# A hybrid decoder block on one core: expert weights in 32 KB ring pieces, the state scan in one tile, constants and squares on VectorE

## The chip, the cores and the metric

The kernel runs on one core of a Trainium2 chip. The metric is the device time of one execution in microseconds (us). Its arithmetic is on TensorE (PE in the profile), VectorE (DVE), ScalarE (ACT) and GpSimd (POOL); SyncE (SP) issues nearly all of its DMAs.

## The reference

256 tokens of 2048 channels, all in float32, pass one decoder layer. What matters of it:

```python
h = rms_norm(x, g1);  proj = h @ w_in              # 1024 + 3*1024 + 2*2048 columns
# state-space mixer: 64 groups of 16 channels, 64 complex states each
x_t = abar * x_{t-1} + bbar @ u_t;  y_t = Re(c @ x_t) + d * u_t
out_s = (z * sigmoid(z @ w_glu)) @ w_bs            # z = gelu(y)
out_a = stick_breaking_attention(q, k, v) @ w_ba   # 8 heads of 128
x2 = x + (sigmoid gates merge out_s and out_a) @ w_out
h2 = rms_norm(x2, g2)
# 32 experts in 4 groups: the best group, in it the best two experts of each token
for e in range(32):
    out += combine[:, e] * (silu(h2 @ w_gate[e]) * (h2 @ w_up[e])) @ w_down[e]
return x2 + out
```

## The kernel before, in words

**The dense stage.** Everything up to `x2` is a list of 200 steps. Each step loads 512 KB of weights (`raw`, issued on SP five steps ahead), splits them into a high part `wh` (a cast on ScalarE) and a low part `wl` (a subtraction on VectorE), and does twelve 128x512 matmuls, `wh` with the high and low part of the activations and `wl` with the high part. All else in this stage is written as generators, `init_stats`, `attention`, `ssm`, `scan`, `gelu` and `heads`; after each step's matmuls the loop at L903 to L934 lets them issue a little, as estimated loads of the engines (`Meter`, L45) allow. Instructions of an engine run in the order in which this loop writes them.

**Three places in it that the change touches.** `init_stats` (L464) sums the squares of `x` over channels: three VectorE reductions leave three partial sums `xsq`, and 12 products with a column of ones (L487) add the partial sums and the partitions at once; each shows as two records. `ssm` (L523) builds the constants of the state space: products of 128x512 between `BC` and small vectors, some issued on GpSimd (`tt` without an engine, L535) and some on VectorE, into `BBD` and `CBD`, and PE transposes `BBD` into `BT`. `scan` (L502) is the recurrence over time. The even times are handled outside; 127 positions remain, and each needs a product of the previous state (real and imaginary parts, times two coefficients) and two additions. The 64 groups of states lie in two tiles `Vs`, and the loop alternates between the halves: two products of 128x64, four additions of 128x32 for a position.

**The expert stage.** The router picks experts; each expert has room for 32 tokens (a rarely used loop handles what overflows). An expert has 16 rows of `wgu` (gate and up) and 8 rows of `wd` (down), a row being 128 partitions x 4 KB, 512 KB. `load_piece` (L856) brings them in pieces of four rows, 2 MB, 16 KB for a partition: 192 pieces for 32 experts. They go round a ring of ten or eleven buffers of 16 KB for a partition, most of which serve as working space of the dense stage earlier. The first seven pieces are issued row by row among the weight loads of the dense stage (`ahead`), the eighth at step 196, and eleven can be in or on their way before the first is used. After that, `gate_up` (L1098) and `down` (L1126) call `load_piece` each time they have used up a piece:

```python
if used[0] <= held.get(j, -1):
    return
held[j] = n
```

For every group of four experts, `gather` (L1058) collects their tokens and `scatter` (L1141) adds the results into `accv`. The last two experts' gate/up weights come first, then their four down pieces, the last of them in two halves; `keep_busy` (L959) puts dummy transposes on PE ahead of those pieces (24 before each group of four gate/up rows, and 24 before each of the first two down pieces).

**The router's start.** When a quarter `n` of the columns of `x2` is done, `x2_tr` (L380) transposes it into a PSUM tile `ps`, ScalarE copies that to `xt` for the router's matmuls, and the squares of `x2` are summed for the norm: by ScalarE for the first three quarters, by VectorE for the fourth. Both write their squares into a scratch tile `junk` that nobody reads.

Of the kernel before, what the change touches and what calls it, by code (L numbers as in the profile page):

```python
# [17 lines left out]
P = 128  # L18
# [64 lines left out]
def hybrid_block(ctx, tc, A, out):  # L83
# [7 lines left out]
    U = {i: ctx.enter_context(tc.tile_pool(name=f"u{i}", bufs=1)) for i in range(11) if i != 6}  # L91

    def unit(i, shape, dt, name):
        return U[i].tile(shape, dt, name=name, tag="u")

    def slot(h, shape, dt, name):
        return hp.tile(shape, dt, name=name, tag=f"h{h}")
# [5 lines left out]
    hp = wctx.enter_context(tc.tile_pool(name="hp", bufs=1))  # L103
# [57 lines left out]
    uge = cq.tile([P, P], F32, name="uge")  # L161
# [5 lines left out]
    nmask = cq.tile([P, P], F32, name="nmask")  # L167
# [149 lines left out]
    def glu_fin(n):  # L317
        def f(a):
            if n == 0:
                ys = unit(7, [P, 2, 8, T], F32R, "ys")  # L320
                S["ys"] = (ys[:, 0], ys[:, 1])
# [58 lines left out]
    def x2_tr(n, t):  # L380
        ps = bg_tile(0)
        for i in range(4):
            k = 4 * n + i
            pe.transpose(ps[:, P * i:P * i + P], S["x2"][:, t, P * k:P * k + P], ident)
        xt = S["xt2"][n, t] = slot((2 * n + t) % 4, [P, 4, P], F32, "xt2")
# [75 lines left out]
    xsq01 = slot(0, [P, 2, T], F32, "xsq01")  # L461
    xsq = [xsq01[:, 0], xsq01[:, 1], slot(1, [P, T], F32, "xsq2")]

    def init_stats():  # L464
# [3 lines left out]
        for at, j, red in ((4, 0, None), (6, 1, (0, 0, 8)), (9, 2, (1, 8, 12)), (12, 3, (2, 12, 16))):  # L468
# [30 lines left out]
    coef = [cq.tile([P, 2, 2, 16], F32, name=f"coef{h}") for h in range(2)]  # L499
    prod = [cq.tile([P, 2, 2, 16], F32, name=f"prod{h}") for h in range(2)]  # L500

    def scan(Vs):  # L502
        at = [1, 1]
        while ("V", 0) not in prog:
            yield 0
        yield -1
        while min(at) < P:
            on = [h for h in range(2) if ("V", h) in prog and at[h] < P]
            for h in on:
                X, c = Vs[h], at[h]  # L510
                vec.tensor_tensor(prod[h], X[:, :, :, c - 1][:, :, None, :].to_broadcast([P, 2, 2, 16]), coef[h], op=OP.mult)
            for k in range(2):
                for h in on:
                    X, c = Vs[h], at[h]
                    vec.tensor_tensor(X[:, :, :, c], X[:, :, :, c], prod[h][:, k], op=OP.add)
            for h in on:
                at[h] += 1
            if len(on) == 1:
                load["vec"] += 0.4
            yield 1 if on else 0  # L520
        prog["scan"] = True

    def ssm():  # L523
        SE = pool
        sm_all = unit(7, [P, 128, 32], F32, "sm")
        sm = sm_all[:, 0:40]
        tw = [sm_all[:, 48 + 16 * i:64 + 16 * i].rearrange("p a b -> p (a b)").rearrange("p (a b) -> p a b", b=16) for i in range(5)]
# [70 lines left out]
        for h in range(2):  # L598
            hs = slice(16 * h, 16 * h + 16)
            SE.tensor_copy(coef[h][:, 0, 0], a2r[:, hs])  # L600
            SE.tensor_copy(coef[h][:, 0, 1], a2i[:, hs])
            SE.tensor_scalar(coef[h][:, 1, 0], a2i[:, hs], -1.0, None, op0=OP.mult)
            SE.tensor_copy(coef[h][:, 1, 1], a2r[:, hs])
# [18 lines left out]
        tt(tw[0], Bi, bc(ci), OP.mult)  # L622
        tt(tw[1], Br, bc(ci), OP.mult)
        yield 0
        tt(t1, Br, bc(cr), OP.mult, vec)
        tt(bre, t1, tw[0], OP.subtract, vec)
        tt(tw[2], Ci, bc(ai), OP.mult)
        yield 0
        tt(t2, Bi, bc(cr), OP.mult, vec)
        tt(bim, t2, tw[1], OP.add, vec)  # L630
        tt(tw[3], Ci, bc(ar), OP.mult)
        yield 0
        tt(tw[0], bim, bc(ai), OP.mult)
        tt(tw[1], bre, bc(ai), OP.mult)
        tt(t1, Cr, bc(ar), OP.mult, vec)
        for g in range(2):
            act.copy(diag(BBD, 0, g), part(bre, g))
            tt(diag(CBD, 2, g), part(t1, g), part(tw[2], g), OP.subtract, vec)
        yield 0
        tt(t2, Cr, bc(ai), OP.mult, vec)  # L640
        for g in range(2):
            act.copy(diag(BBD, 1, g), part(bim, g))
            vec.scalar_tensor_tensor(diag(CBD, 3, g), part(t2, g), -1.0, part(tw[3], g), op0=OP.mult, op1=OP.subtract)
        yield 0
        tt(t1, bre, bc(ar), OP.mult, vec)
        for g in range(2):
            tt(diag(BBD, 2, g), part(t1, g), part(tw[0], g), OP.subtract, vec)
            act.copy(diag(CBD, 0, g), part(Cr, g))
        yield 0
        tt(t2, bim, bc(ar), OP.mult, vec)  # L650
        for g in range(2):
            tt(diag(BBD, 3, g), part(t2, g), part(tw[1], g), OP.add, vec)
            act.mul(diag(CBD, 1, g), part(Ci, g), -1.0)
# [11 lines left out]
        CB = cq.tile([P, 16, 32], F32, name="CB")  # L665
# [17 lines left out]
        Vs = [unit(7 + h, [P, 2, 16, P], F32, f"Vs{h}") for h in range(2)]  # L683
        gens.append(scan(Vs))
        gens.append(gelu())
        for b in range(8):
# [7 lines left out]
            for i in range(2):  # L694
                src = tiles[i].rearrange("p (a r c) -> p r a c", a=2, r=2)
                j = 4 * (b % 4) + i
                act.copy(Vs[b // 4][:, :, j:j + 3:2], src)
# [6 lines left out]
        for b in range(8):  # L704
            pp = [bg_tile(0), bg_tile(0)]
            X = Vs[b // 4]
            for par in (1, 0):
                ps = pp[par]
                for si in range(3):
                    for j in range(4):  # L710
# [6 lines left out]
                        elif par == 1:  # L717
                            pe.matmul(ps[js, 0:P], CBD[:, si - 1, 4 * b + j], X[:, si - 1, i],
                                      start=False, stop=(si == 2), tile_position=(0, 32 * j))
                        else:  # L720
                            pe.matmul(ps[js, 1:P], CBD[:, 1 + si, 4 * b + j], X[:, si - 1, i, 0:P - 1],
# [5 lines left out]
    def gelu():  # L727
# [4 lines left out]
        zz = unit(9, [P, 2, 8, T], F32R, "zz")  # L732
# [28 lines left out]
    def attention():  # L761
# [20 lines left out]
        QT = [slot(h, [P, 2, T], F32, f"qkT{h}") for h in range(8)]  # L782
# [11 lines left out]
        AT = unit(4, [P, 2, 2, 2, 3, P], F32, "AT")  # L794
        gens.insert(0, heads(QT, AT[:, 0], (0, 2)))
        gens.insert(1, heads(QT, AT[:, 1], (4, 6)))

    def heads(QT, at, firsts):
# [4 lines left out]
        for h0 in firsts:  # L803
# [32 lines left out]
            for i in range(2):  # L836
                y = slot(h0 + i, [P, 2, T], F32R, f"ya{h0 + i}")
# [8 lines left out]
    ring = [U[i] for i in (10, 8, 9, 2, 7, 4, 3, 1)]  # L846
    used = [0]
    held = {}
    ahead = []
    pieces = [(e, i) for e in range(NE - 2) for i in range(6)]  # L850
    pieces += [(e, i) for e in (NE - 2, NE - 1) for i in range(4)]
    pieces += [(e, i) for i in (4, 5) for e in (NE - 2, NE - 1)]
    ptile = {}
    nextp = [0]

    def load_piece():  # L856
        n = nextp[0]
        if n >= len(pieces):
            return
        j = n % 11 if n < 22 else (n - 22) % 10  # L860
        j += n >= 22 and j > 5
        if used[0] <= held.get(j, -1):
            return
        held[j] = n
        e, i = pieces[n]
# [414 lines left out]
```

## Time and profile before

| | us |
|---|---|
| median of 3 runs | 1563.29 |
| lowest and highest | 1561.04, 1563.48 |
| the profiled execution's own time | 1564.15 |
| its span in the profile | 1562.4 |

| engine | busy us | share of the span |
|---|---|---|
| PE | 1263.4 | 81% |
| VectorE | 541.0 | 35% |
| ScalarE | 451.4 | 29% |
| GpSimd | 55.9 | 4% |

516.91 MB move in the span. All shares are averages over two stages that differ: the dense stage up to 633 us and the expert stage after it. So they are read by stretches: which engine is full in each, and what ended the idle time of the others.

### The profile page before, as it was taken

Reading aid. Unit: us, or ns where it says so; the run is one execution under the profiler, and the core shown is the slowest. Engines: PE = TensorE matmul, PEld = TensorE weight load, DVE = VectorE, ACT = ScalarE, POOL = GpSimd, SP = SyncE. Lnnn points to the kernel's source line nnn. Section 1 sums busy time; section 2 is a strip of 40 time slices with the busy share of each in tenths; the row PEclk is TensorE's granted clock in tenths of the full one; section 3 lists DMA queues with packets and bytes.
Section 4 is the critical chain, followed back from the end, with each engine's and each line's share of the span. In section 5 each row is a group of like instructions: output and inputs, shape, how many; then the busy total and the mean of one; then the engine's idle time right before and its main releaser. Section 6 shows DMA issues by size and latency. Waiting matters only on the chain.

```text
span 1562.4 us, 25151 instructions
## 1 busy us (share of the span) xinstructions
PE 1263.4 (81%) x10662; PEld 862.0 (55%) x10662; DVE 541.0 (35%) x1338; ACT 451.4 (29%) x768; POOL 55.9 (4%) x111
## 2 busy tenths in 40 slices
PE   9999999999999999987558557657657657657697
PEld 7878888888879888644224224323324323323364
DVE  7746878898856744302002002002002002001001
ACT  5645567554455444120100100110110110110101
POOL 6700000000000000000000000000000000000000
PEclk9999999999999999999879878878988779878899
DMA  8545655566657886999999999999999999999996
GB/s 266 175 131 159 195 153 158 163 193 189 202 191 256 277 281 229 379 427 427 427 427 428 428 426 426 428 428 427 427 427 427 426 428 428 426 428 427 426 426 242
DMA packets 65108, 516.91 MB, mean 331 GB/s; under 512 B 7905, under 2 KB 8161, under 8 KB 41441
## 3 DMA queue, kind: packets, MB, share of 16 engines
q1 hardware_dynamic: 64704, 515.21, 83.9%
q8 instruction: 86, 1.41, 0.4%
q14 instruction: 30, 0.24, 0.0%
q10 hardware_dynamic: 288, 0.06, 0.0%
HBM read 513.14 MB, written 2.10 MB: 330 GB/s over the span
## 4 chain that ended last, share of the span: by engine, by line
DMA 53%; PE 43%; DVE 2%; ACT 1%; issue 1%; SPq 0%; DVEq 0%
PE acc L77 38%; DMA ew<-wgu 33%; DMA ew<-wd 19%; PE bga L77 3%; PE bgb L77 2%; DVE wl L77 1%; ACT XY L77 0%; DMA raw<-win 0%; DVE R L77 0%; ACT wh L77 0%; DVE BC L77 0%; DVE Vs L77 0%; ACT AT L77 0%; ACT uy L77 0%; DVE prod L77 0%
## 5 line engine op out<-in xcount | busy, mean ns | idle before, releaser
L77 PE MATMUL acc<-ew,XY 128*32 128x256 f32 x4096 | 306.1, 451 | 159.3 <-DMA ew<-wgu 159.1
L77 PEld LDWEIGHTS acc<-ew,XY 128*32 128x32 f32 x4096 | 140.8, 125 | 308.1 <-DMA ew<-wgu 175.0
L77 DVE TENSOR_TENSOR wl<-raw,wh 128x1024 fp32r<-128x1024 f32 (+1 forms) x201 | 244.9, 1222 | 146.9 <-ACT wh L77 145.8
L77 ACT CAST wh<-raw 128x1024 fp32r<-128x1024 f32 x199 | 208.5, 1052 | 180.0 <-PE acc L77 121.3
L77 DVE TENSOR_TENSOR sg<-sg,acc 128x128 f32<-128x128 f32 x32 | 9.2, 288 | 642.3 <-ACT sg L77 642.3
L77 PE MATMUL acc<-ew,hT 128*32 128x256 f32 (+1 forms) x2080 | 155.0, 450 | 76.7 <-DMA ew<-wd 46.1
L77 ACT COPY XY<-acc 32x256 f32<-32x256 f32 (+1 forms) x260 | 93.7, 360 | 224.7 <-PE acc L77 222.2
L77 PEld LDWEIGHTS acc<-ew,hT 128*32 128x32 f32 x2080 | 76.5, 126 | 144.8 <-issue 69.8
L77 PE MATMUL acc<-wh,xh 128*128 128x512 f32 x512 | 145.6, 401 | 1.6 <-ACT wh L77 0.9
L77 PE MATMUL acc<-wh,xl 128*128 128x512 f32 x512 | 140.8, 392 | 0.0
L77 PE MATMUL acc<-wl,xh 128*128 128x512 f32 x512 | 140.4, 391 | 0.0
L77 ACT ACTIVATE sg<-acc 128x128 f32<-128x128 f32 x32 | 8.9, 278 | 402.0 <-PE acc L77 402.0
L77 PEld LDWEIGHTS acc<-wh,xl 128*128 128x128 f32 x512 | 97.0, 189 | 21.0
L77 PEld LDWEIGHTS acc<-wl,xh 128*128 128x128 f32 x512 | 96.7, 189 | 20.5
L77 PEld LDWEIGHTS acc<-wh,xh 128*128 128x128 f32 x512 | 93.9, 190 | 21.1 <-ACT wh L77 1.9
L77 PE MATMUL acc<-XY,sc 128*128 128x512 f32 x128 | 66.4, 663 | 14.5 <-ACT XY L77 14.5
L77 DVE TENSOR_TENSOR Vs<-Vs,prod 128x32 f32<-128x32 f32 x508 | 76.7, 221 | 0.0
L77 DVE TENSOR_TENSOR accv<-accv,acc 128x512 f32<-128x512 f32 x56 | 38.5, 687 | 97.6 <-PE acc L77 97.6
L77 PE MATMUL bga<-SL,x 128*128 128x128 f32 x512 | 63.5, 280 | 10.3 <-DVE SL L77 10.3
L77 PEld LDWEIGHTS bga<-SL,x 128*128 128x128 f32 x512 | 59.0, 192 | 22.9 <-DVE SL L77 15.8
L77 PE MATMUL acc<-wh,m 128*128 128x512 f32 x256 | 64.6, 392 | 0.0
L77 DVE TENSOR_TENSOR prod<-Vs,coef 128x64 f32<-128x64 f32 x254 | 56.0, 262 | 0.0
(222 smaller groups left out, 984.1 us busy)
## 6 DMA issues: line engine op xcount, KB each, us to landing
ew<-wgu SPq DMA_DIRECT2D x123, 2048.0 KB, 39.1
ew<-wd SPq DMA_DIRECT2D x61, 2048.0 KB, 39.1
raw<-win SPq DMA_DIRECT2D x127, 512.0 KB, 4.1
raw<-wout SPq DMA_DIRECT2D x32, 512.0 KB, 4.5
ew<-wgu SPq DMA_DIRECT2D x20, 512.0 KB, 6.2
raw<-wba SPq DMA_DIRECT2D x16, 512.0 KB, 4.6
raw<-wbs SPq DMA_DIRECT2D x16, 512.0 KB, 5.3
raw<-wglu SPq DMA_DIRECT2D x8, 512.0 KB, 4.9
```

Of the source, the lines that this page charges most:

```text
L77: return f(out, *args, **kw)
```

## The change

**The expert ring.** The working buffers of the dense stage become "homes": A, B and C of 32 KB for a partition (two former 16 KB buffers each) and Z, V, S, T and X of 16 KB. A fourth 32 KB home W opens when the dense stage's weight buffers are freed. The first pieces follow a written table; from the third expert's end on, every piece has eight rows, 4 MB, 32 KB for a partition, and W, A, B, C take turns. Before, a partition's bytes of a piece lay in 16 KB runs, now in 32 KB runs (86 such DMAs). A home is refilled when its rows are used (`holds`, `where`, `used`); the table of the first pieces refills A and B by halves. The number of 2 MB units that can be in before the first is used is eleven, as before; the ring after that holds 16 MB instead of 20 MB.

**The rest.** The scan works on one tile: for a position one product of 128x128 and two additions of 128x64. The constants are computed on VectorE alone, in six more 128x512 products. Two additions on VectorE sum the three partial sums of squares, and four products with ones remain. The scratch results of `x2_tr` go into the PSUM tile `ps`, and several tiles move to other buffers.

```diff
-    U = {i: ctx.enter_context(tc.tile_pool(name=f"u{i}", bufs=1)) for i in range(11) if i != 6}
+    for n, us in (("A", (7, 8)), ("B", (9, 2)), ("C", (3, 4)), ("Z", (0,)), ("V", (1,)), ("S", (10,)), ("T", (6,)), ("X", (5,))):
+        H[n] = ctx.enter_context(tc.tile_pool(name=f"home{n}", bufs=1))
...
-        junk = slot(4 + (2 * n + t) % 4, [P, 512], F32, "junk")
...
-            act.activation(junk, xs, AF.Square, accum_out=ssq[:, t, n:n + 1])
+            act.activation(ps, xs, AF.Square, accum_out=ssq[:, t, n:n + 1])
...
-            vec.scalar_tensor_tensor(junk, xs, 1.0, xs, op0=OP.mult, op1=OP.mult, accum_out=ssq[:, t, n:n + 1])
+            vec.scalar_tensor_tensor(ps, xs, 1.0, xs, op0=OP.mult, op1=OP.mult, accum_out=ssq[:, t, n:n + 1])
...
+                if red[0]:
+                    vec.tensor_tensor(xsq[0], xsq[0], xsq[red[0]], op=OP.add)
...
-                for j in range(3):
-                    pe.matmul(ps[:, 2 * o + t:2 * o + t + 1], xsq[j][:, tt], ones[:, 0:1], start=(j == 0), stop=(j == 2))
+                pe.matmul(ps[:, 2 * o + t:2 * o + t + 1], xsq[0][:, tt], ones[:, 0:1], start=True, stop=True)
...
+    def scan(X):
+        while ("V", 1) not in prog:
+            yield 0
...
+        for c in range(1, P):
+            vec.tensor_tensor(prod, X[:, :, :, c - 1][:, :, None, :].to_broadcast([P, 2, 2, 32]), coef, op=OP.mult)
             for k in range(2):
+                vec.tensor_tensor(X[:, :, :, c], X[:, :, :, c], prod[:, k], op=OP.add)
...
-        tt(tw[0], Bi, bc(ci), OP.mult)
-        tt(tw[1], Br, bc(ci), OP.mult)
+        tt(t1, Br, bc(cr), OP.mult, vec)
+        tt(t2, Bi, bc(ci), OP.mult, vec)
+        tt(bre, t1, t2, OP.subtract, vec)
...
-    pieces = [(e, i) for e in range(NE - 2) for i in range(6)]
...
+    EARLY = 6
+    pieces = [(0, 0, 8, "A", 0), (0, 8, 16, "B", 0), (0, 16, 20, "S", 0), (0, 20, 24, "T", 0), (1, 0, 8, "C", 0),
+              (1, 8, 12, "V", 0), (1, 12, 16, "W", 0), (1, 16, 20, "W", 4), (1, 20, 24, "A", 0), (2, 0, 4, "A", 4),
+              (2, 4, 8, "B", 0), (2, 8, 12, "B", 4), (2, 12, 16, "S", 0), (2, 16, 24, "C", 0)]
+    first = len(pieces)
+    for e in range(3, NE):
+        for r in range(0, 16, 8):
+            pieces.append((e, r, r + 8))
+        if e < NE - 2:
+            pieces.append((e, 16, 24))
+    pieces += [(NE - 2, 16, 24), (NE - 1, 16, 24)]
+    pieces = [p if n < first else (*p, "WABC"[(n - first) % 4], 0) for n, p in enumerate(pieces)]
...
     def load_piece():
...
-        if used[0] <= held.get(j, -1):
-            return
-        held[j] = n
...
+        if any((h, at + r) in holds for r in range(hi - lo)):
+            return False
...
+        if n < EARLY - 1:
+            for r in range(lo, hi):
+                ahead.append(lambda r=r: sp.dma_start(tl[:, r - lo], source(e, r, r + 1)[:, 0]))
+        elif n < last - 1:
+            sp.dma_start(tl, source(e, lo, hi))
         else:
...
+            sp.dma_start(tl[:, 0:4], source(e, 16, 20))
+            S["tail", e] = tl
+            if n == last:
+                sp.dma_start(S["tail", NE - 2][:, 4:8], source(NE - 2, 20, 24))
+                for c0, cw in ((0, LSPLIT), (LSPLIT, 1024 - LSPLIT)):
+                    sp.dma_start(tl[:, 4:8, c0:c0 + cw], source(e, 20, 24)[:, :, c0:c0 + cw])
...
+    def used(e, r):
+        for k in [k for k, v in holds.items() if v == (e, r)]:
+            del holds[k]
+        if r % 4 == 3:
+            while load_piece():
+                pass
```

**Where instructions move.** The first place is VectorE where the constants are built, around 60 to 83 us. `BC` holds the constants' inputs and, before, their products; now the products lie in `homeA`; `sm` holds small vectors, and `wl` is the low part of a dense step. Before:

```order
L77 TENSOR_TENSOR wl<-raw,wh 128x1024
L77 TENSOR_TENSOR BC<-BC,sm 128x512
L77 TENSOR_TENSOR BBD<-BC,sm 64x32x16 x2
L77 TENSOR_TENSOR wl<-raw,wh 128x1024 x3
L77 TENSOR_TENSOR CB<-dmask,dsk 128x512
```

Now:

```order
L77 TENSOR_TENSOR CBD<-homeA 64x32x16 x2
L77 TENSOR_TENSOR wl<-raw,wh 128x1024
L77 TENSOR_TENSOR homeA<-homeA 128x512 x2
L77 TENSOR_TENSOR wl<-raw,wh 128x1024
L77 SCALAR_TENSOR_TENSOR CBD<-homeA 64x32x16 x2
L77 TENSOR_TENSOR wl<-raw,wh 128x1024 x3
L77 TENSOR_TENSOR CB<-dmask,dsk 128x512
```

`BBD`, which PE waits for, was the last constant on VectorE and is now ahead of `CBD`.

The second place is VectorE at the start of the scan, at about 149 us before (`Vs_1082` and `Vs_1083` are the two halves, `prod` the products, `k_118` the tile that holds product and coefficients after the change, `homeA` the one tile of the states). Before, two positions:

```order
L77 TENSOR_TENSOR prod_224<-Vs_1082,coef_222 128x64
L77 TENSOR_TENSOR prod_225<-Vs_1083,coef_223 128x64
L77 TENSOR_TENSOR Vs_1082<-Vs_1082,prod_224 128x32
L77 TENSOR_TENSOR Vs_1083<-Vs_1083,prod_225 128x32
L77 TENSOR_TENSOR Vs_1082<-Vs_1082,prod_224 128x32
L77 TENSOR_TENSOR Vs_1083<-Vs_1083,prod_225 128x32
L77 TENSOR_TENSOR prod_224<-Vs_1082,coef_222 128x64
```

Now:

```order
L77 TENSOR_TENSOR homeA<-homeA,k_118 128x64 x2
L77 TENSOR_TENSOR wl<-raw,wh 128x1024
L77 TENSOR_TENSOR k_118<-homeA,k_118 128x128
L77 TENSOR_TENSOR homeA<-homeA,k_118 128x64 x2
L77 TENSOR_TENSOR k_118<-homeA,k_118 128x128
L77 TENSOR_TENSOR homeA<-homeA,k_118 128x64 x2
L77 TENSOR_TENSOR wl<-raw,wh 128x1024
```

A position is three instructions, each needing the one before it; it was six, in two chains. The scan's 127 positions stand between the splits of some 78 steps now (44 to 121), before of some 103 (41 to 143).

The third place is the end of SP's queue, the last expert pieces. Before:

```order
L873 DMA ew<-wgu 128x4096 x8
L873 DMA ew<-wd 128x4096 x3
L873 DMA ew<-wd 128x4x512 x2
```

Now:

```order
L886 DMA ewA<-wgu 128x8192
L886 DMA ewB<-wgu 128x8192
L886 DMA ewC<-wgu 128x8192
L886 DMA ewW<-wgu 128x8192
L889 DMA ewA<-wd 128x4096
L889 DMA ewB<-wd 128x4096
L892 DMA ewA<-wd 128x4096
L894 DMA ewB<-wd 128x4x512 x2
```

The gate/up rows of the last two experts come in four transfers of eight rows instead of eight of four; the down pieces stay as they were.

## Rows read from the trace of the kernel before

**Rows 1.** Part 2 of the page: busy tenths in 40 slices of 39 us

```profile
PE   9999999999999999987558557657657657657697
DMA  8545655566657886999999999999999999999996
```

**Rows 2.** Windows: stretch, us, busy us (x instructions) by engine, PEclk, DMA share, GB/s

```profile
80.00:85.00 5.00, 2.04 (x10) 1.80 (x10) 4.39 (x5) 1.27 (x2) 0.00 (x0) 0.79 0.50 164
85.00:90.00 5.00, 5.00 (x30) 4.41 (x28) 1.23 (x1) 2.72 (x5) 0.00 (x0) 0.87 0.41 116
163.00:393.00 230.00, 229.86 (x1062) 191.62 (x1062) 195.67 (x661) 133.34 (x159) 0.00 (x0) 1.00 0.57 175
499.00:502.00 3.00, 3.00 (x15) 2.49 (x14) 1.24 (x2) 1.05 (x1) 0.00 (x0) 1.00 1.02 415
900.00:1400.00 500.00, 326.29 (x3585) 163.78 (x3581) 42.55 (x81) 58.73 (x170) 0.00 (x0) 0.83 1.01 427
```

**Rows 3.** Waits of PE in the dense stage: us in total, times, longest

```profile
PE bga L77 <- DVE BBD L77: 3.0, 1, 3.0
```

**Rows 4.** Timeline of PE: start us, duration us, instructions in a row

```profile
49.27 2.81 PE L77 MATMUL bga<-ones,xsq 128*128 128x1 f32 x24
```

**Rows 5.** Groups of VectorE by form: xcount | busy us, mean ns | idle before

```profile
L77 DVE TENSOR_TENSOR wl<-raw,wh 128x1024 fp32r<-128x1024 f32 x199 | 243.5, 1227 | 146.8 <-ACT wh L77 145.8
L77 DVE TENSOR_TENSOR Vs<-Vs,prod 128x32 f32<-128x32 f32 x508 | 76.7, 221 | 0.0
L77 DVE TENSOR_TENSOR prod<-Vs,coef 128x64 f32<-128x64 f32 x254 | 56.0, 262 | 0.0
L77 DVE TENSOR_TENSOR gate<-acc,gate 128x512 f32<-128x512 f32 x16 | 10.9, 689 | 1.9 <-PE acc L77 1.9
L77 DVE TENSOR_TENSOR sg<-sg,acc 128x128 f32<-128x128 f32 x32 | 9.2, 288 | 642.3 <-ACT sg L77 642.3
L77 DVE TENSOR_TENSOR BC<-BC,sm 128x512 f32<-128x512 f32 x8 | 8.1, 1007 | 1.4 <-POOL sm L536 1.3
```

**Rows 6.** Windows again, 163 to 393 us, of single tiles: wl, then Vs

```profile
163.00:393.00 230.00, 83.26 (x304) 57.21 (x305) 92.91 (x77) 1.00 0.57 175
...
163.00:393.00 230.00, 0.00 (x0) 0.00 (x0) 82.18 (x534) 0.00 (x0) 1.00 0.57 175
```

**Rows 7.** Timeline of VectorE: the state scan, then the router

```profile
149.93 0.45 DVE L77 TENSOR_TENSOR prod<-Vs,coef 128x64 f32<-128x64 f32 x2
150.29 0.60 DVE L77 TENSOR_TENSOR Vs<-Vs,prod 128x32 f32<-128x32 f32 x4
150.80 1.22 DVE L77 TENSOR_TENSOR wl<-raw,wh 128x1024 fp32r<-128x1024 f32 x1
...
640.18 0.48 DVE L77 TENSOR_TENSOR R<-R,R 128x64 f32<-128x64 f32 x2
```

**Rows 8.** Timeline of VectorE and ScalarE where the router begins

```profile
634.72 0.69 DVE L77 SCALAR_TENSOR_TENSOR junk<-x 128x512 f32<-128x512 f32 x1
634.94 0.59 ACT L77 COPY xt<-bga 128x512 f32<-128x512 f32 x1 [0.41 <-PE bga L77]
```

**Rows 9.** Part 6 of the page: DMA issues, xcount, KB each, us to landing

```profile
ew<-wgu SPq DMA_DIRECT2D x123, 2048.0 KB, 39.1
```

**Rows 10.** Chain that ended last: start us, us, what

```profile
1384.43 39.09 DMA ew<-wd
1487.92 39.91 DMA ew<-wgu
1527.88 1.98 PE acc L77 x32
```

**Rows 11.** Timeline of PE: end of a group's gate/up, then the last gate/up

```profile
1454.56 1.93 PE L77 MATMUL acc<-ew,XY 128*32 128x256 f32 x32
...
1524.97 2.84 PE L77 MATMUL acc<-ident 128*128 128x128 f32 x24
1527.88 1.93 PE L77 MATMUL acc<-ew,XY 128*32 128x256 f32 x32
```

More of the change, by code (lines that the diff above doesn't have):

```diff
@@ L496, in init_stats @@
         yield 0.8
[L499 to L504, printed above, removed]
+    coef = shaped(k2[:, 256:384], [P, 2, 2, 32])
+    prod = shaped(k2[:, 384:512], [P, 2, 2, 32])
+    def scan(X):
+        while ("V", 1) not in prog:
             yield 0
         yield -1
[L507 to L511, printed above, removed]
-            for k in range(2):
[L513 to L520, printed above, removed]
+        for c in range(1, P):
+            vec.tensor_tensor(prod, X[:, :, :, c - 1][:, :, None, :].to_broadcast([P, 2, 2, 32]), coef, op=OP.mult)
+            for k in range(2):
+                vec.tensor_tensor(X[:, :, :, c], X[:, :, :, c], prod[:, k], op=OP.add)
+            load["vec"] += 0.3
+            yield 1
         prog["scan"] = True
@@ L639, in ssm @@
+        for g in range(2):
+            act.copy(diag(CBD, 0, g), part(Cr, g))
+        tt(t1, Cr, bc(ar), OP.mult, vec)
+        tt(t2, Ci, bc(ai), OP.mult, vec)
         yield 0
[L640 removed]
         for g in range(2):
[L642 to L643 removed]
+            tt(diag(CBD, 2, g), part(t1, g), part(t2, g), OP.subtract, vec)
+            act.mul(diag(CBD, 1, g), part(Ci, g), -1.0)
@@ L644, in ssm @@
         yield 0
-        tt(t1, bre, bc(ar), OP.mult, vec)
+        tt(t1, Cr, bc(ai), OP.mult, vec)
+        tt(t2, Ci, bc(ar), OP.mult, vec)
+        yield 0
         for g in range(2):
[L647 to L653, printed above, removed]
+            vec.scalar_tensor_tensor(diag(CBD, 3, g), part(t1, g), -1.0, part(t2, g), op0=OP.mult, op1=OP.subtract)
@@ new lines, in hybrid_block, with source @@
+    first = len(pieces)
[6 more added lines that the diff above has]
+    pieces = [p if n < first else (*p, "WABC"[(n - first) % 4], 0) for n, p in enumerate(pieces)]
+    last = len(pieces) - 1
+    holds, room, where, ahead, nextp = {}, {}, {}, [], [0]
+    def source(e, lo, hi):
+        return A["wgu"][e][:, lo:hi] if hi <= 16 else A["wd"][e][:, lo - 16:hi - 16]
@@ L874, in load_piece @@
-        ptile[e, i] = tl
-        nextp[0] += 1
+        if n > last:
+            return False
+        e, lo, hi, h, at = pieces[n]
+        if any((h, at + r) in holds for r in range(hi - lo)):
+            return False
+        if h not in room:
+            room[h] = H[h].tile([P, 4 if h in "STV" else 8, 1024], F32, name="ew" + h, tag="u")
+        tl = room[h][:, at:at + hi - lo]
+        for r in range(lo, hi):
+            where[e, r] = room[h][:, at + r - lo]
+            holds[h, at + r - lo] = e, r
@@ L954, in hybrid_block @@
     rt = ctx.enter_context(tc.tile_pool(name="rt", bufs=1, reuse_waits="tile"))
-    for i in range(3):
-        ring.append(ctx.enter_context(tc.tile_pool(name=f"w{i}", bufs=1, reuse_waits="tile")))
+    H["W"] = ctx.enter_context(tc.tile_pool(name="homeW", bufs=1, reuse_waits="tile"))
     def keep_busy(n):
@@ L1049, in overflow @@
         vec.tensor_copy(oli, ps[0:1, 2:35])
+    while load_piece():
+        pass
     XY = unit(0, [P, 2, 16, P], F32, "XY")
@@ L1127, in down @@
         i = e % 4
-        w = ptile[e, 4 + c0 // 1024]
+        w = [where[e, 16 + 4 * (c0 // 1024) + j] for j in range(4)]
         n4 = cw // 4
```

150 lines of the change are left out of this document (69 added, 81 removed).

## The prediction

> **What bounds the kernel now.** I read the page's slices first [rows 1]: PE is full for the first 16 slices, then falls to 5 to 8 tenths, while the DMA engines go from 5 to 8 tenths to full. So there are two kernels: up to 633 us PE sets the time, and only a wait or an instruction on PE can be gained; after it the weight stream does. The windows [rows 2] confirm it: from 163 to 393 us PE is busy 229.86 of 230 us, from 900 to 1400 us only 326 of 500, with the DMA share at 1.01 and 427 GB/s. Next come the waits of PE in the dense stage [rows 3], where one of 3.0 us, on `BBD`, stands out, and the chain that ended last [rows 10]: DMA of expert pieces up to 1527.83, then PE alone to the end of the span at 1562.4. The end is that last gate/up landing plus 34.6 us of PE.
>
> What comes in before the expert stage is eleven 2 MB units with and without the change. Time gained or lost in the dense stage therefore moves the start of the saturated stream and passes on in full. The sum is made against the profiled execution's 1564.15; the median is 0.86 lower.
>
> **Squares of x.** 24 records of products with ones take 2.81 us of PE [rows 4]; 8 remain, so 16 x 2.81/24 = **-1.9**. The two additions of 128x256 on VectorE stand right behind the reductions, ahead of the products at 49.27; beside a full PE they cost nothing, and without that cover some 0.4 each, by size between the `sg` and the `gate` row [rows 5].
>
> **Constants.** Six 128x512 products come to VectorE: 6 x 0.689 (the `gate` row) = 4.1 us. The eight there took 1.007 each [rows 5] beside GpSimd's, 0.318 more than `gate`; without those 2.5 us return. The surplus of 1.6 is spread over ten steps instead of seven, beside splits of 1.227 in steps of about 2.99 us (230/77, [rows 6]): room. `BBD` now precedes `CBD`, and the transposes come three steps later, so the wait of 3.0 [rows 3] goes: **-3.0**. Bounds: 0 if the wait returns on another constant, -3.0 since no more is lost there. The granted clock read 0.79 around that wait and 0.87 in the five busy microseconds behind it [rows 2]; full clock there gives (1 - 0.87) x 5 = **-0.6**.
>
> **Scan.** From 163 to 393 us, 77 splits pass and VectorE is busy 195.67 us [rows 2]; splits are 92.91 of it and the scan 82.18 [rows 6], which leaves 20.6 for attention. The changed scan lies beside 78 splits, nearly the same stretch, with 127 positions of T each. VectorE is full when 92.9 + 20.6 + 127T = 230, at T = 0.917 us. T is one product of 128x128 (0.288, the `sg` row) and two additions of 128x64 (0.222: 0.221 at 32 columns and 0.262 for the 64-column `prod`, [rows 5]; the two dependent `R` additions, which take 0.48 together, say 0.22 with a gap of 0.04, [rows 7]). The sum is 0.732 without gaps and 0.85 with three of 0.04. Before, a position cost 0.87 at the start of the scan (149.93 to 150.80, [rows 7]), in six instructions that overlapped, since there were two chains; now nothing overlaps but the splits. At 0.85 VectorE is busy 221.5 of 230 us, a cover of 8.5 us that attention uses unevenly: I take **+1.0**. Bounds: 0, and at gaps of 0.10, which no row shows, T = 1.03 and 127 x 0.115 = +14.6. If the cover goes, the split `wl` is late, and PE waits for it.
>
> **Product outputs.** The products of the scan's results with `CBD` move to earlier steps, same count: 0 on a full PE.
>
> **Scratch in PSUM.** The last square sum on VectorE began at 634.72, while the copy out of the same PSUM tile ran on ScalarE from 634.94 to 635.53 [rows 8]. Writing into that tile, it must wait for the copy: 635.53 + 0.04 - 634.72 = **+0.85**. The norm and the router follow; the weight stream runs on during them, but the homes it is to refill come free later, so I count all of it; 0 is the lower bound.
>
> **Row size.** Eight 2 MB pieces are in flight at 39.1 us each [rows 9], 4.89 us a piece. 86 transfers with 32 KB runs carry 172 such units, 841 us. What is a run's own cost? At 499 to 502 us the stream is full with 4 KB runs: share 1.02 at 415 GB/s, so one run holds one of 16 engines 4096 x 16 x 1.02/415 = 161 ns. With 16 KB runs (share 1.01, 427 GB/s) it is 620 ns [rows 2]. The line through both has 8 ns of fixed cost a run. At 32 KB that is 1232 ns against 2 x 620 = 1240: 0.65% of 841 us, **-5.4**. Bounds: 0, and twice it, -11. The first 4 KB window is short and shared with the dense loads, and gives the largest uncertainty.
>
> The Trainium skill ("DMA: Bandwidth & Descriptors", "Why small descriptors are slow") gives about 3 cycles of overhead per packet beside one 32-byte beat a cycle. By it a 32 KB run saves 3 of 2 x 515 cycles, 0.29%, and this term would be -2.5, an estimate from that page. The rows speak for more: 16 KB runs are 3.9% faster than 4 KB ones by (427/1.01)/(415/1.02), where the page's count gives 1.7%. The same page's ceiling of 435 GB/s ("Where 436 GB/s comes from") would leave at most 1.9% above 427.
>
> **Smaller ring.** With four homes a transfer is issued when the piece four before it is used up; the stream idles only if PE is three pieces, 3 x 9.8 = 29 us, behind a landing. The worst place is the start of a group of four experts: at 1423.5 the last down piece landed [rows 10] and PE finished the next expert's gate/up, landed at 1423.5 + 4 x 4.89 = 1443.1, at 1456.5 [rows 11], having waited on the scatter between. The first eight of those rows landed at 1433.3 and are used up before the last four begin at 1454.6, at most 21 us later: 8 us of slack or more, **0**.
>
> **End.** The last gate/up piece has eight rows and lands at once. Before, one group of four rows (1.93) stood behind the landing; now a second comes with its 24 dummy transposes (2.84, [rows 11]): **+4.8**. The down pieces behind it have their homes free and land as early as before.
>
> Sum: -1.9 - 3.0 - 0.6 + 1.0 + 0.85 - 5.4 + 4.8 = -4.25; 1564.15 - 4.25 = 1559.9, and with the median's 0.86, **1559.0**.
>
> **The rivals.**
> (a) Longer runs move no faster: either the chip cuts them into the same packets, so that the change is not what it says, or the engines are at their rate already. For it: share 1.01 at 427 GB/s in every window of the stage. Without the -5.4 the rest sums to +1.15: 1564.4, no measurable change. The page's rule lies between this case and the forecast, and has no chance of its own. Chance 0.28.
> (b) The other side: the scan's single chain makes VectorE the bound of the dense stage. Its place is steps 44 to 121, it decides from T = 0.917 (gaps over 0.06), and it outweighs the other gains from 1.0 + 4.25 = 5.25 us on, T = 0.96. At T = 1.03, gaps of 0.10, it costs 14.6 instead of 1.0: 1572.6. At T = 0.99, 9.3 us and 1567. Against it: the gap of 0.04 in [rows 7]; for it: VectorE would be 96% full even so. Chance 0.12.
> (c) The ring starves at the seven group starts. It decides if PE is over 8 us later than now at each; 3 us lost at each gives 21 us, 1580. Against it, the slack worked out above. Chance 0.04.
> (d) It gains more: the dummy transposes before the last four rows fall into a wait that is there anyway, so that the end costs 1.9 instead of 4.8 (1556.1), or a run saves twice what the line says (1553.6). Chance 0.13.
>
> **How the numbers follow.** The forecast has 0.43. A measurement of this kernel tells about 0.2%, 3.1 us, from no change: faster is below 1560.2, slower above 1566.4. The forecast lies 1.2 us below that line, and I give three quarters of it, 0.32, to faster and 0.11 to the same; (d) adds 0.13 to faster and some of (a), where the rest turns out better, 0.03. The same gets 0.11 + 0.23 from (a) + 0.02 from a mild (b), 0.36; slower gets the rest of (a), (b) and (c), 0.16. Faster has 0.48. The range takes the forecast, (d) and (a) with a mild (b): 1553.5 to 1567.5, leaving out the ends of (b) and (c) and the bound of -11.
>
> **What would show it.** Right: 8 records of ones with squares, under 1.1 us; no wait on `BBD`; PE waits on `wl` under 2 us in all; a scan position of about 0.85; the stage's GB/s near 430 and a 4 MB transfer at 9.72 us instead of 9.78; two groups of four rows, 6.7 us, behind the last gate/up landing. Wrong: 427 GB/s as before means (a); waits of PE on `wl` between 160 and 400 us mean (b); a DMA share under 1.0 at group starts means (c).

## The result, and the profile after

The changed kernel takes 1579.77 us (median; 1579.46 to 1580.74, 4 runs) against 1563.38 of the kernel before (1561.04 to 1564.91, 4 runs). The ratio is 1.0107, 95% interval 1.0094 to 1.0121: 1% slower, where 1559.0 and a small gain had been forecast, with a range up to 1567.5. The profiled execution took 1579.46 us, its span 1577.8, 15.4 more than before.

Where did it go? Three marks divide the span: the last addition of the dense stage (`x<-x,acc`), the landing of the last gate/up piece, and the end.

| | dense stage ends | last gate/up lands | span | dense to landing | landing to end |
|---|---|---|---|---|---|
| before | 633.5 | 1527.8 | 1562.4 | 894.3 | 34.6 |
| after | 650.0 | 1539.0 | 1577.8 | 889.0 | 38.8 |

The first mark is the start of that addition, 633.51 and 649.99 in the two traces; the landing before is in [rows 10]. The dense stage lost 16.5 us; the stream won 5.3, the end lost 4.2. The slices of the page after, to compare with [rows 1], show no other picture, a full PE in front and a full DMA behind:

```profile
PE   9999999999999999976756757756756656756797
DMA  8644644546457888799999999999999999999995
```

The windows of the changed kernel, to set beside [rows 2]; columns as there:

```profile
80.00:85.00 5.00, 5.00 (x23) 4.14 (x23) 4.27 (x6) 2.69 (x3) 0.00 (x0) 1.00 0.52 166
163.00:393.00 230.00, 218.13 (x983) 176.73 (x982) 208.15 (x450) 124.50 (x150) 0.00 (x0) 0.99 0.53 159
900.00:1400.00 500.00, 323.12 (x3609) 169.86 (x3609) 42.56 (x81) 60.18 (x174) 0.00 (x0) 0.82 1.00 430
```

At 80 to 85 us PE is busy all the time at full clock, where 2.04 of 5.00 us and 0.79 stood before: the constants' part works. From 163 to 393 us PE lost 12 of 230 us, which it had not before. From 900 to 1400 us the stream shows 430 GB/s instead of 427. What PE waits for in the dense stage now, in place of [rows 3] (the view of waits; total, times, longest):

```profile
PE acc L77 <- DVE wl L77: 8.8, 10, 2.5
PE acc L77 <- ACT wh L77: 5.6, 5, 1.5
```

So the splits are late (before, PE waited nowhere on `wl` and 0.9 us on `wh`). The tile view of the same 230 us, `wl` and then the tile of the states, answers to [rows 6]:

```profile
163.00:393.00 230.00, 78.70 (x280) 51.49 (x280) 84.96 (x70) 0.99 0.53 159
...
163.00:393.00 230.00, 0.00 (x0) 0.00 (x0) 104.05 (x330) 0.00 (x0) 0.00 (x0) 0.99 0.53 159
```

70 splits pass where 77 did: a step takes 230/70 = 3.29 us instead of 2.99. The states take 104.05 us for 330 instructions, 110 positions, 0.946 each without their gaps. The forms of the scan on VectorE, beside [rows 5]:

```profile
L77 DVE TENSOR_TENSOR homeA<-homeA,k 128x64 f32<-128x64 f32 x254 | 72.1, 284 | 8.8
L77 DVE TENSOR_TENSOR k<-homeA,k 128x128 f32<-128x128 f32 x127 | 48.4, 381 | 2.6
```

and their order in time, beside [rows 7]:

```profile
198.50 0.38 DVE L77 TENSOR_TENSOR k<-homeA,k 128x128 f32<-128x128 f32 x1
198.91 0.61 DVE L77 TENSOR_TENSOR homeA<-homeA,k 128x64 f32<-128x64 f32 x2
199.55 0.39 DVE L77 TENSOR_TENSOR k<-homeA,k 128x128 f32<-128x128 f32 x1
199.98 0.62 DVE L77 TENSOR_TENSOR homeA<-homeA,k 128x64 f32<-128x64 f32 x2
```

From 198.50 to 199.55 a position takes 1.05 us; the next one takes 1.08. The prediction had 0.85, with 0.288 for the product and 0.222 for an addition; they take 0.381 and 0.284. The gaps are as it had them (0.03 from 198.88 to 198.91, some 0.1 in a position).

### The profile page after: what moved, and what is told of

It is laid out like the page before. It is cut to its first block, busy times and chain, and to the rows that moved or that the text cites. A ratio compares the mean times of both kernels' runs of the same rounds, so it can differ in the third digit from the quotient of the medians.

```text
span 1577.8 us, 24538 instructions
## 1 busy us (share of the span) xinstructions
PE 1264.0 (80%) x10646; PEld 865.4 (55%) x10646; DVE 544.7 (35%) x965; ACT 450.2 (29%) x768; POOL 49.8 (3%) x101
## 5 line engine op out<-in xcount | busy, mean ns | idle before, releaser
L77 PE MATMUL acc<-ewA,XY 128*32 128x256 f32 x992 | 78.2, 482 | 49.7 <-DMA ewA<-wgu 49.7
L77 PE MATMUL acc<-ewC,XY 128*32 128x256 f32 x1024 | 76.2, 456 | 37.4 <-DMA ewC<-wgu 37.4
L77 PE MATMUL acc<-ewB,XY 128*32 128x256 f32 x1024 | 72.1, 442 | 32.7 <-DMA ewB<-wgu 32.6
L77 PEld LDWEIGHTS acc<-ewA,XY 128*32 128x32 f32 x992 | 40.0, 137 | 87.3 <-DMA ewA<-wgu 38.5
L77 PE MATMUL acc<-ewW,XY 128*32 128x256 f32 x992 | 65.2, 413 | 15.1 <-DMA ewW<-wgu 15.1
L77 PEld LDWEIGHTS acc<-ewC,XY 128*32 128x32 f32 x1024 | 35.8, 130 | 71.9 <-DMA ewC<-wgu 40.8
L77 DVE TENSOR_TENSOR homeA<-homeA,k 128x64 f32<-128x64 f32 x254 | 72.1, 284 | 8.8
L77 PEld LDWEIGHTS acc<-ewB,XY 128*32 128x32 f32 x1024 | 36.2, 127 | 66.5 <-DMA ewB<-wgu 37.8
```

Source lines behind the costliest of these rows:

```text
L77: return f(out, *args, **kw)
```

## The experiments

Theory S: the scan's position is dearer than 0.917 us, so that VectorE holds back the splits of the dense stage. Rival H: the homes do it, with loads that wait for working tiles. Theory L speaks of the rate of the stream (length of a run), theory E of the end.

**The scan in two halves.** The changed kernel with only the scan put back to two interleaved halves, in the one tile. The estimate that goes with them spreads the scan out again, so chain and density change together here; the next two kernels take them apart:

```diff
-            vec.tensor_tensor(prod, X[:, :, :, c - 1][:, :, None, :].to_broadcast([P, 2, 2, 32]), coef, op=OP.mult)
+            for h in range(2):
+                hs = slice(16 * h, 16 * h + 16)
+                vec.tensor_tensor(prod[:, h], X[:, :, hs, c - 1][:, :, None, :].to_broadcast([P, 2, 2, 16]), coef[:, h], op=OP.mult)
...
-            load["vec"] += 0.3
```

> The changed kernel, with the state scan alone put back to two interleaved halves (six instructions a position, in the one tile; the estimates then spread it over some 103 steps again). Theory S, the scan's single chain makes VectorE the bound (a position takes 1.05 to 1.08 us in the trace of the changed kernel, 127 of them between 78 splits, over the 0.917 at which VectorE is full): the dense stage falls from 648.6 to about 630, a position to 0.87 to 0.92, PE's waits on wl and wh between 100 and 440 us from 12 us to under 1, and the time to 1579.8 - 18 = 1561 to 1563. Rival H, the homes cost the time (loads held until working tiles are free, pieces of eight rows): the dense stage stays near 648 and the time above 1575.

1555.72 us, ratio to before 0.9955 (0.9939 to 0.9972). Rival H is out. The dense stage ends 24.7 us earlier than in the changed kernel (the row of its last addition):

```profile
625.29 0.69 DVE L77 TENSOR_TENSOR x<-x,acc 128x512 f32<-128x512 f32 x1 [0.68 <-PE acc L77]
```

and from 163 to 393 us (tile views of `wl` and the states) 78 splits pass, with 90 positions at 0.924:

```profile
163.00:393.00 230.00, 83.10 (x304) 57.07 (x304) 93.61 (x78) 1.00 0.56 176
...
163.00:393.00 230.00, 0.00 (x0) 0.00 (x0) 83.18 (x540) 0.00 (x0) 0.00 (x0) 1.00 0.56 176
```

The expected 18 us were too few; this kernel is also 8.2 us ahead of the one before at that mark, where the prediction's gains in the dense stage came to 5.5. Of the 24.7 us, PE's idle time up to the mark makes 14.4 (17.2 against 2.8). The other 10.3 are in its busy time (632.8 against 622.5): products right behind a wait take longer, four of them 1.19 or 1.20 us instead of 1.07, and the granted clock read 0.86 and 0.80 in the two windows from 330 to 340 us, around its longest wait. These 10.3 were not divided further.

**The scan spread out, and the scan packed.** The first keeps the one tile and raises its estimated load (`load["vec"] += 0.3` becomes `+= 0.5`), 93 splits instead of 78. The second keeps the two halves and lowers theirs (`load["vec"] -= 0.297`), 77 splits.

> The changed kernel with the scan still in one tile, but its estimated load a position raised by 0.2, so that its 127 positions stand beside 93 splits instead of 78. Theory S in the form that only the density is at fault (127 x 1.07 = 136 us of scan, 93 splits at about 1.13 = 105 and 25 of attention make 266 of 93 x 2.99 = 278 us): VectorE just keeps up, the dense stage falls to 632 to 637, the time to 1563 to 1568. Theory S in the form that a chain of dependent instructions holds back each split wherever it stands: less than a third of the loss returns, 1574 to 1580. Rival H: no change, 1579.8.

1572.05 us (ratio 1.0054, 1.0037 to 1.0071): a third of the 24 us returns, less than the first form of the theory wanted and more than the second. Its dense stage ends at 641.2, and the waits of PE there are of another kind:

```profile
PE acc L77 <- ACT zz L77: 7.6, 1, 7.6
PE acc L77 <- ACT wh L77: 2.9, 3, 1.5
```

PE stands 7.6 us for the gelu's result `zz`, for which it does not wait before. The scan is not late for it: its last product on VectorE starts at 419.25 here and at 439.64 with the two halves. What differs is the place of the gelu. Here PE's products with the scan's results go two groups to a step, up to 463.31, and the gelu follows in one piece, with nothing for PE beside it. With the two halves those products stand close together, and the gelu goes between them in quarters. The casts into `zz` on ScalarE, all four here, then the first with the two halves:

```profile
470.87 2.42 ACT L77 CAST zz<-homeB 128x512 fp32r<-128x512 f32 x4 [1.31 <-DVE homeB L77]
453.11 0.62 ACT L77 CAST zz<-homeB 128x512 fp32r<-128x512 f32 x1
```

So the estimated load moves more than the scan, and this kernel is no clean test of the density. It shows that the waits on `wl` all but go (0.3 us in all) when the one tile is spread over 93 splits.

> The scan in two halves as in e1_halves, but packed as densely as in the changed kernel: its estimated load a position lowered by 0.297, 127 positions between splits 44 and 120. Theory S1, what costs is the VectorE time of a position: 0.92 a position (82.18/89 in the kernel before) makes 127 x 0.92 + 92.9 + 20.6 = 230 of 230 us, VectorE just full, so some 3 to 8 us of e1's gain are lost: 1558 to 1564. Theory S2, the density itself costs (a split stands behind too much scan work, however short its instructions): at least 15 us lost, 1571 or more.

1568.14 us (1.0027, 1.0017 to 1.0037), between the two theories. The tile views from 163 to 393 us:

```profile
163.00:393.00 230.00, 79.08 (x287) 53.16 (x287) 89.13 (x74) 1.00 0.55 169
...
163.00:393.00 230.00, 2.57 (x64) 1.50 (x64) 101.06 (x666) 0.00 (x0) 0.00 (x0) 1.00 0.55 169
```

666 instructions are 111 positions at 0.91, as cheap as S1 said, yet only 74 splits pass and the dense stage ends 11.0 us later than with the same instructions spread out:

```profile
636.25 0.69 DVE L77 TENSOR_TENSOR x<-x,acc 128x512 f32<-128x512 f32 x1 [0.68 <-PE acc L77]
```

VectorE's busy time in this window is 209.4 us here and 208.15 in the changed kernel, and both are late; it is 197.1 in the two halves spread out and 195.67 before [rows 2], and both are on time. So of 24.7 us, 11.0 come with the density while a position is cheap, and 13.7 more when it is dearer at the same density, in one chain instead of two. Taken in another order the shares differ, as the next kernel shows.

**Why a position is dear.** In the one tile the 64 values of a position lie 512 bytes apart in a partition. This kernel lays them side by side and changes nothing else:

```diff
-        Vs = shaped(pair["A"], [P, 2, 32, P])
+        Vs = shaped(pair["A"], [P, P, 2, 32]).rearrange("p t r j -> p r j t")
```

> The changed kernel with the one tile of states laid out by time first, so that the 64 values of a position lie side by side in a partition instead of 512 bytes apart; same instructions, same order, same 78 splits. Theory P, the position is dear because of the stride (product 0.381 where a contiguous one of 128x128 takes 0.288, additions 0.284 where contiguous ones of 128x64 take 0.222): product about 0.29, additions about 0.22, a position 0.85, VectorE has cover again, the dense stage ends some 18 to 24 us earlier, time 1556 to 1562; PE's products that read the states, now with a stride, and ScalarE's copies into it could take some of it back. Rival Q, the durations come from the size alone or from the broadcast operand: product and additions stay at 0.38 and 0.28, time 1577 to 1582.

1586.25 us (1.0142, 1.0125 to 1.0159): the time missed, the durations as theory P had them. The forms on VectorE are those the prediction had assumed:

```profile
L77 DVE TENSOR_TENSOR homeA<-homeA,k 128x64 f32<-128x64 f32 x254 | 57.2, 225 | 8.7
L77 DVE TENSOR_TENSOR k<-homeA,k 128x128 f32<-128x128 f32 x127 | 36.6, 288 | 2.5
```

Size and broadcast are the same, so the stride costs 0.093 on the product and 0.059 on an addition. In the dense stage this is worth most of what was lost. The last product of the scan, in the changed kernel and then here:

```profile
396.32 0.37 DVE L77 TENSOR_TENSOR k<-homeA,k 128x128 f32<-128x128 f32 x1
376.57 0.28 DVE L77 TENSOR_TENSOR k<-homeA,k 128x128 f32<-128x128 f32 x1
```

The first ones start at 141.94 and 141.04, so the scan, with the same single chain beside the same splits, takes 235.5 us from first to last instead of 254.4: 18.9 us by the stride. PE's waits in the dense stage fall from 8.8 and 5.6 us to

```profile
PE acc L77 <- ACT wh L77: 3.6, 4, 1.5
PE acc L77 <- DVE wl L77: 0.3, 1, 0.3
```

But now PE's products read the states with a stride. The timeline of PE, sixteen of them in the changed kernel, then here:

```profile
418.09 0.64 PE L77 MATMUL bga<-homeA,CBD 128*32 128x128 f32 x16
```

```profile
411.70 2.06 PE L77 MATMUL bga<-homeA,CBD 128*32 128x128 f32 x16
```

2.06 us instead of 0.64, 1.42 more for each of 16 such groups: some 22.7 us, more than the scan won, and the dense stage ends at 654.8 instead of 650.0. The Trainium skill ("SBUF — State Buffer", "Specifications (TRN2)") says that SBUF has lines of 16 bytes and that each step to a new line costs; the rows agree, for both engines, and this rule spoke against the prediction's choice of a row. Only these two layouts were tried, so no run shows at which stride the cost begins.

**The squares alone, the constants alone.** Each put into the kernel before.

```diff
+                if red[0]:
+                    vec.tensor_tensor(xsq[0], xsq[0], xsq[red[0]], op=OP.add)
...
-                for j in range(3):
-                    pe.matmul(ps[:, 2 * o + t:2 * o + t + 1], xsq[j][:, tt], ones[:, 0:1], start=(j == 0), stop=(j == 2))
+                pe.matmul(ps[:, 2 * o + t:2 * o + t + 1], xsq[0][:, tt], ones[:, 0:1], start=True, stop=True)
```

> The kernel before with only the squares changed (two additions on VectorE, four products with ones instead of twelve). Theory C, the run of 24 one-column records costs its own 1.9 us and also drops PE's clock behind it (granted clock 0.72 from 50 to 55 us and 0.94 to 60 in the kernel before, 1.00 in the changed one): 1562.4 - 1.9 - 1.7 = 1558.8, with 1.00 in both windows. Rival, only the 1.9 us: 1560.5 and a clock below 1 still there.

1563.06 us, no change (0.9993, 0.9984 to 1.0003). The clock came out as expected: window 50 to 55 us of the kernel before, then two windows of this one,

```profile
50.00:55.00 5.00, 5.00 (x26) 4.36 (x27) 2.44 (x9) 2.37 (x4) 4.67 (x10) 0.72 0.58 193
```

```profile
50.00:55.00 5.00, 4.92 (x22) 3.79 (x23) 2.90 (x10) 3.81 (x6) 4.67 (x10) 1.00 0.62 188
75.00:80.00 5.00, 3.69 (x16) 2.44 (x14) 4.73 (x7) 2.22 (x4) 0.00 (x0) 1.00 0.56 168
```

1.00 instead of 0.72. But then, at 75 to 80 us, PE idles 1.3 us, and its waits are

```profile
PE bga L77 <- DVE BBD L77: 3.0, 1, 3.0
PE acc L77 <- DVE wl L77: 1.8, 2, 1.2
```

PE arrives earlier at the constants, which are not ready earlier; all that was won is waited away there, and the dense stage ends at 633.5 as before. The time was neither expectation; of theory C the clock's part is shown, and not that it reaches the end.

The constants (the lines of the change, with their six products on VectorE):

```diff
-        tt(tw[0], Bi, bc(ci), OP.mult)
-        tt(tw[1], Br, bc(ci), OP.mult)
+        tt(t1, Br, bc(cr), OP.mult, vec)
+        tt(t2, Bi, bc(ci), OP.mult, vec)
+        tt(bre, t1, t2, OP.subtract, vec)
...
```

> The kernel before with only the constants changed (all on VectorE, products for BBD first). The 3.0 us wait of PE for BBD goes, and with it the clock of 0.79 and 0.87 from 80 to 90 us: 1562.4 - 3.6 = 1558.8. Rival, VectorE's six more products make a split late: a wait on wl of 1 to 3 us appears between 60 and 85 us, and the time is 1560 to 1562.

1557.69 us (0.9957, 0.9941 to 0.9974); the dense stage ends at 628.3, 5.2 earlier, where 3.6 had been expected; the other 1.6 was not traced. No wait on `BBD`, and the windows where it had been are busy at full clock:

```profile
80.00:85.00 5.00, 5.00 (x23) 4.14 (x23) 3.31 (x5) 4.28 (x6) 0.00 (x0) 1.00 0.41 143
85.00:90.00 5.00, 5.00 (x29) 4.28 (x29) 4.05 (x5) 1.99 (x4) 0.00 (x0) 1.00 0.66 210
```

The edit changes engine and order of the constants at once; which of the two ends the wait was not separated. The kernel with two halves, which has both parts, is 8.2 us ahead at the mark. That the other 3.0 are the squares, which count once the constants are out of the way, is argued and not shown: this kernel differs in its homes and buffers too.

**The length of a run.** The changed kernel with each 4 MB piece in two transfers of four rows (16 KB runs); then with one transfer of 4 MB again, but into homes with a gap of 32 bytes in the middle (16 KB runs, the same number of transfers):

```diff
-            sp.dma_start(tl, source(e, lo, hi))
+            for r in range(lo, hi, 4):
+                sp.dma_start(tl[:, r - lo:r - lo + 4], source(e, r, r + 4))
```

```diff
-            whole = H[n].tile([P, 8192], F32, name=f"home{n}", tag="u")
+            whole = H[n].tile([P, 2, 4104], F32, name=f"home{n}", tag="u")
...
+                sp.dma_start(S["room", h], source(e, lo, hi).rearrange("p (j k) c -> p j (k c)", j=2))
```

> The changed kernel with every 4 MB piece issued as two transfers of four rows, 16 KB runs, into the same homes; nothing else changes. Theory L, a run has a fixed cost of 8 to 11 ns: 5 to 6 us slower in the stream (427 GB/s instead of 430), but the last gate/up rows then land in fours; they stand behind PE work of the rows before, so that the end takes back up to 4.3: between 1579.8 + 1 and 1579.8 + 6. Rival, the 430 GB/s come from the homes or from fewer transfers and not from the run length: 430 GB/s stays, and the time is 1575 to 1580.

> The changed kernel with a gap of 32 bytes in the middle of each 32 KB home, so that an expert piece is still one transfer of 4 MB but lies in two 16 KB runs for each partition. Theory L, the length of a run sets the rate: 427 GB/s from 900 to 1400 us as in e3_rows16, the last gate/up landing some 6 us later than in the changed kernel, time 1583 to 1587. Rival, the number or size of the transfers sets it: 430 GB/s as in the changed kernel and 1578 to 1581.

1581.06 us and 1583.65 us (ratios 1.0117 and 1.0119, each in its expected range). The window of the steady stream in each:

```profile
900.00:1400.00 500.00, 318.53 (x3577) 162.09 (x3577) 42.57 (x81) 60.17 (x174) 0.00 (x0) 0.85 1.01 427
```

```profile
900.00:1400.00 500.00, 323.53 (x3601) 170.09 (x3593) 42.51 (x81) 60.02 (x174) 0.00 (x0) 0.82 1.01 428
```

From the end of the dense stage to the last landing they take 895.3 and 894.5 us, the changed kernel 889.0 and the one before 894.3. So it is the run length, 5.5 to 6.3 us, as theory L had it, and the number of transfers does nothing that shows. The other traces mostly bear it out: 894.1 and 894.6 in the two kernels made from the one before (16 KB), 888.7, 888.8 and 890.1 with halves, packed halves and time first (32 KB). The spread-out scan's 892.1 is the exception, and was not explained.

A third way, two transfers of 64 partitions each, was to hold the run at 32 KB and double the transfers:

```diff
-            sp.dma_start(tl, source(e, lo, hi))
+            for p0 in (0, 64):
+                sp.dma_start(tl[p0:p0 + 64], source(e, lo, hi)[p0:p0 + 64])
```

> The changed kernel with each 4 MB piece issued as two transfers of 64 partitions: runs stay 32 KB, the number of transfers is that of e3_rows16. Theory L, the length of a run sets the rate: 430 GB/s from 900 to 1400 us as in the changed kernel, time 1578 to 1582. Rival, the number or the size of the transfers sets it: 427 GB/s as in e3_rows16, and the last gate/up landing some 6 us later.

2476.33 us (1.5844). It says nothing of runs, since the rate halves (window 1000 to 2000 us):

```profile
1000.00:2000.00 1000.00, 358.58 (x3564) 184.11 (x3568) 42.57 (x81) 57.26 (x166) 0.00 (x0) 0.67 1.00 212
```

212 GB/s with the engines' share at 1.00. The Trainium skill ("SBUF — State Buffer", "Door 1: The DMA port swizzle (why `[64,N]` ≈ `[32,N]`)") has partitions 0 to 63 reach half of the ports and 64 to 127 the other half; 212 against 430 agrees if the two transfers move one after the other, which no run here shows.

**The end.** Of the changed kernel, the issue of the last gate/up piece on SP with its time to landing, 1507.46 + 31.5 = 1539.0, and PE behind it:

```profile
1507.46 0.33 SPq L886 DMA_DIRECT2D ewW<-wgu  x1
...
ewW<-wgu SPq DMA_DIRECT2D x1, 4096.0 KB, 31.5
```

```profile
1539.05 1.93 PE L77 MATMUL acc<-ewW,XY 128*32 128x256 f32 x32
1540.91 2.84 PE L77 MATMUL acc<-ident 128*128 128x128 f32 x24
1543.68 1.93 PE L77 MATMUL acc<-ewW,XY 128*32 128x256 f32 x32
```

As foreseen, two groups and a set of dummies follow the landing. In fours for experts 30 and 31 alone:

```diff
+            step = 4 if e >= NE - 2 else 8
+            for r in range(lo, hi, step):
+                sp.dma_start(tl[:, r - lo:min(r + step, hi) - lo], source(e, r, min(r + step, hi)))
```

> The changed kernel with only the last four gate/up pieces (experts 30 and 31) issued as two transfers of four rows each. Theory E, the eight rows that land at once leave PE 38.8 us behind the last landing instead of 34.6: those 4.3 us return, 1575 to 1576. Rival, PE is behind anyway because of the dummy transposes: it stays at 1579 to 1580.

1580.15 us, nothing gained: the time is the rival's. The last piece is issued at 1508.22 and lands 30.4 later, at 1538.6, but its products start only at 1544.21. PE's timeline shows where it fell behind:

```profile
1499.48 3.64 PE L77 MATMUL acc<-ewW,hT 128*32 128x256 f32 x32 [3.65 <-DMA ewW<-wd]
1508.08 2.84 PE L77 MATMUL acc<-ident 128*128 128x128 f32 x24
1510.85 1.93 PE L77 MATMUL acc<-ewA,XY 128*32 128x256 f32 x32
```

Expert 29's down piece lands as eight rows; its first half takes 3.64 us where 1.93 is usual (granted clock 0.50, the lower level of 1.2 GHz, after 3.65 us of waiting), the second 3.43, both are done at 1508.08, and after a set of dummies the first gate/up group of expert 30 starts at 1510.85. From there groups and dummies take 4.64 us, the stream 4.9: PE never catches up. So that piece goes in fours too, on the kernel with the two halves (`e >= NE - 2 or (e == NE - 3 and lo == 16)`):

> The kernel of e1_halves (scan in two halves) with the last down piece of expert 29 and the gate/up pieces of experts 30 and 31 issued as transfers of four rows. In e4_split_last PE came late into the tail: eight rows of expert 29's down piece landed at once at 1499.35, and with 4.77 us of products and dummies for each 4.9 us of stream it never caught up. Theory E2: with that piece in fours too PE follows the landings again, 34.6 us lie behind the last landing instead of 38.8, and 1555.7 falls to 1551 to 1552. Rival: the rows behind the landing stay at 38 to 39 us, 1555 to 1556.

1549.40 us, ratio to before 0.9910 (0.9894 to 0.9927), faster than both kernels and 1.6 better than theory E2 had. PE is on time, the second half of the down piece takes 1.93, and the last group starts at its landing, with 33.7 us from there to the end of the span at 1547.3:

```profile
1474.47 1.93 PE L77 MATMUL acc<-ewW,hT 128*32 128x256 f32 x32 [1.91 <-DMA ewW<-wd]
1476.33 2.84 PE L77 MATMUL acc<-ident 128*128 128x128 f32 x24
1479.27 1.93 PE L77 MATMUL acc<-ewA,XY 128*32 128x256 f32 x32
1513.60 1.93 PE L77 MATMUL acc<-ewW,XY 128*32 128x256 f32 x32
```

The kernel with every piece in two transfers of four rows says the same: its last piece lands at 1544.7, with 34.0 us from there to the end of its span at 1578.7.

## Why the prediction was wrong, step by step

**Scan**: the step that failed, +1.0 predicted and +24.7 measured (650.0 against 625.3 with the two halves). Two of its choices were wrong. It priced strided instructions by contiguous rows, `sg` and `R`, although [rows 5] had the scan's own `prod`, 0.262 for 64 columns where contiguous additions of 64 take 0.225 (time first); 0.949 plus gaps came of 0.732 plus gaps. Laid out contiguously the scan is 18.9 us shorter. And it called VectorE full at 230 of 230 us, while the runs with 208 and 209 were late already, and with the two cheap halves packed 11.0 us were lost; what leaves the other 20 us idle was not tried. What failed was thus the price T and the point from which VectorE holds PE back. By its own formula, T of 1.06 gives 1558.0 + 127 x 0.143 = 1576.2, most of the way to 1579.77: rival (b) had the mechanism and the place. Its gap of 0.10 stood in for the stride, so that its T of 1.03 came near the measured one by luck.

**Squares**: -1.9 predicted. Alone 0, since the time is waited away at the constants. With the constants' part perhaps -3, as 8.2 - 5.2 = 3.0, a difference between kernels that differ in more than this. The prediction had not seen that the clock's dip goes too, nor that the gain hangs on the wait behind it.

**Constants**: -3.6 with the clock, measured -5.2 alone. Right in its mechanism: the wait and the dip are gone, and the products on VectorE take 0.699 each in the changed kernel, close to the 0.689 of its price. The size was too small by 1.6, cause open.

**Scratch in PSUM**: right to the hundredth in its place. The timeline where the router begins, beside [rows 8]:

```profile
649.99 0.69 DVE L77 TENSOR_TENSOR x<-x,acc 128x512 f32<-128x512 f32 x1 [0.68 <-PE acc L77]
651.43 0.59 ACT L77 COPY xt<-bga 128x512 f32<-128x512 f32 x1 [0.42 <-PE bga L77]
652.05 0.70 DVE L77 SCALAR_TENSOR_TENSOR bga<-x 128x512 f32<-128x512 f32 x1 [0.24 <-ACT xt L77]
```

The last square sum starts 2.06 us after the last addition instead of 1.21, +0.85, having waited for ScalarE's copy. It was not undone alone. That it reaches the end is not shown: together with the ring it costs 0.2 to 1.0 (below), so the sum may have counted too much here.

**Row size**: -5.4 predicted, 5.5 to 6.3 measured; rival (a) is out. The line through the 4 KB and 16 KB rows held. The rule of the Trainium skill that was weighed there ("DMA: Bandwidth & Descriptors", "Why small descriptors are slow (HBM only)") gives an estimate of -2.5, less than half of it.

**Smaller ring**: 0, right. With 16 KB runs in the same homes the way from the dense stage's end to the last landing is 894.5 us with transfers of 4 MB and 895.3 with 2 MB, before it was 894.3, so ring and scratch cost 0.2 to 1.0 together, where rival (c) wanted some 21; it is out.

**End**: +4.8 predicted, +4.2 measured; the two groups are there as foreseen. What it had not seen is that expert 29's down piece, which lands as eight rows too, already puts PE behind transfers of four rows, so that splitting the last pieces alone does not undo it.

The sum of the parts: -8.2 + 24.7 - 5.3 + 4.2 = +15.4, the change of the span. Without the scan's part the forecast of 1558.0 would have come within 2.3 us of the 1555.72 measured, in part by luck, since constants and squares gave 8.2 at the mark and not 5.5.

## What to carry to other kernels

Price an instruction by a row with its own access pattern: same size with another stride is another price, on VectorE and on PE. Before merging two interleaved chains into one of longer instructions, look at how busy the engine is in that stretch: here, with PE following step by step, PE lost 0.2 of 230 us at most with VectorE busy for 85 or 86%, 3.2 at 88% (spread out), and 5.7 and 11.9 at 91%. These are five kernels and no rule, since the two at 91% lost unlike amounts, and the kernel with time first lost 2.5 at 82%, where its scan ends inside the stretch. A gain ahead of a wait is only a gain when the wait goes too, so test parts of a change alone and together.

## What the runs showed of the hardware

PE's granted clock was lower after a long run of one-column products. Behind 24 records of them in 2.81 us [rows 4] it read 0.72 over 5 us, between its two levels of 1.2 and 2.4 GHz. Behind 8 in 0.97 us it read 1.00 in every kernel that has 8. In the changed kernel:

```profile
49.26 0.97 PE L77 MATMUL bga<-ones,qt 128*128 128x1 f32 x8
```

A stride of 512 bytes takes 0.284 instead of 0.225 us on a 128x64 addition of VectorE; on PE a stride of 256 bytes in the moving operand takes sixteen products from 0.64 to 2.06 us. And the stream of loads, cut into transfers of 64 partitions, ran at 212 GB/s where transfers into 128 ran at 430.
